# Start of a hybrid encoder trunk on one core: the first weights move to ScalarE's DMA queue, small loads to POOL's, and TensorE's first instructions are put in a written order

## The chip, the cores and the metric

The kernel runs on one core of a Trainium2 chip. The metric is the time of one execution on the device in microseconds (us); where several runs are given, the median counts. A profile of one execution stands beside the times.

## What is computed

Two post-norm layers of an encoder over 512 positions of width 1024. Each layer adds a token mixer and then a squared-ReLU MLP, both with a LayerNorm of `alpha * x + sublayer(x)`. The mixer of the first layer is a bidirectional gated DeltaNet, that of the second a bidirectional GLA.

```python
def reference(x, ...):
    for i in range(DEPTH):                      # DEPTH = 2
        if i % 2 == 0: m = _mixer_gdn(x, a_w_in, a_conv, a_alog, a_dt_bias, a_norm_g, a_w_out)
        else:          m = _mixer_gla(x, b_w_in, ...)
        x = _layernorm(DEEPNORM_ALPHA * x + m, ln1_g[i], ln1_b[i])
        x = _layernorm(DEEPNORM_ALPHA * x + _sq_relu_mlp(x, mlp_w1[i], mlp_w2[i]), ln2_g[i], ln2_b[i])
    return x
```

Only the start of the first mixer matters here. It projects x with `a_w_in` (1024 x 4128): 8 heads with q, k, v and z of 128 columns each, and 32 last columns that give the gates. From these columns come `beta` (a sigmoid) and the decay `g = -exp(a_log) * softplus(. + dt_bias)`; q, k and v go through a short convolution with `a_conv`, and a gated delta rule runs over them in both directions.

## The kernel before, in words

All products of the projections are made in three matmuls of the type fp32r: each operand is split into a high part and the rest (`split`, L85: ScalarE casts `wh`, VectorE subtracts to get `wl`), and `mm3` (L111) adds high x high, high x low and low x high into one bank. x is wanted with its width on the partitions, so its four tiles of 128 positions (`xt`, 512 KB each, rows of 4 KB) are transposed on TensorE (`xpose`, L144 to L156): per tile two banks of four 128 x 128 transposes, then ScalarE's copy to `xth` and VectorE's subtraction to `xtl`. The banks come in turn from the PSUM pools `ac` (2 banks), `ch` (2) and `tp` (1).

`gdn` (L965) first calls `load_x` (L453), which issues the four loads of x on SP and traces the transposes of all four tiles. Then `GdnConst` (L803) is built: triangular masks `cum` on POOL, zeroed tiles `pz` on VectorE, then `gates` (L893). `gates` loads two small broadcasts on ScalarE's queue (`bia` and `coef`, 64 bytes to each partition), the 32 gate columns `bst` (128 KB) and the first head's k columns (512 KB, here called `k0`) on SP's; the splits of both stand behind the last copy of x on their engines (`issue_after`). `proj_halves` (L123) then projects positions 0 to 255 with both sets of weights and afterwards positions 256 to 511: 24 matmuls of 256 columns into the bank `bap` (gates) and 24 into `pjk` (k), per half. Four transposes (`gtp`, L917) and some twenty small operations of VectorE and ScalarE make the gate rows from `bap`. Behind `gates` come the convolution weights `cw` (60 KB, one transpose, L826) and `norm_g` on ScalarE's queue, and masks on POOL that the heads' solves read.

Then the heads are run in a software pipeline: while head i is projected, head i-1 is solved and head i-2 recurs. Head 0's k is already in `pjk`, so the next product is its q (`pjq`), whose weights are the third to be loaded.

What sets the order: a scheduler of the framework places the instructions of each engine at build time, by priority in the order of the program and by what it thinks is ready; each engine then runs its list strictly in order. `in_order` (L58) fixes the order of one engine's instructions within a block to that of the program. Loads of weights go through the pool `wst`, which has three buffers: `bst`, `k0` and the weights of `pjq` fill it, the fourth load waits until `bst` has been split. `c.dma` (L47) always issues on SP.

Of the kernel before, what the change touches and what calls it, by code (L numbers as in the profile page):

```python
# [8 lines left out]
F32 = mybir.dt.float32  # L9
# [3 lines left out]
AF = mybir.ActivationFunctionType  # L13
# [4 lines left out]
P = 128  # L18
S = 512
D = 1024  # L20
KT = D // P
NT = S // P
# [6 lines left out]
class Ctx:  # L29


    def __init__(self, tc, nc, pools):
        self.tc, self.nc = tc, nc
        self.const, self.big, self.wst, self.whl, self.small = pools
        nc_ = nc
        self.ident = self.const.tile([P, P], F32, name="ident")
        make_identity(nc_, self.ident[:, :])

        self.bias = {}
        for i, v in enumerate((LN_EPS, RMS_EPS, -0.5 * math.log(P))):  # L40
            self.bias[v] = self.const.tile([P, 1], F32, name=f"bias{i}")
            nc.vector.memset(self.bias[v], v)
        self.xth = self.xtl = self.xt = None
        self.dma_i = 0
        nc.scalar.preload_act_table_set("natural_log_exp_and_others")
# [78 lines left out]
                     k == 0, k == KT - 1)  # L124
        return ps

    def proj_halves(self, specs):

        out = [self.bank([P, S], F32, name=name, tag=tag) for _, name, tag in specs]
        for hf in range(2):  # L130
            sl = slice(hf * 256, hf * 256 + 256)
            for ps, ((wh, wl), _, _) in zip(out, specs):
                n = wh.shape[-1]
                for k in range(KT):
                    self.mm3(ps[:n, sl], wh[:, k, :], wl[:, k, :], self.xth[:, k, sl], self.xtl[:, k, sl],
                             k == 0, k == KT - 1)
        return out
# [120 lines left out]
def mlp(c, w1, w2, g, b, out=None, extra=None):  # L258
# [12 lines left out]
    with c.banks(pj=2, X=2, Y=2, Z=2), tc.tile_pool(name="mlp", bufs=2) as pool:  # L271
# [176 lines left out]
            second(gi, h, a, nxt)  # L448
            h, a = nh, nxt.a if more else None
        last(G - 1, h)  # L450


def load_x(c, x, tags):  # L453
    c.new_xt()
    c.new_x()
    for t in range(NT):
        c.dma(c.xt[t], x[t * P:(t + 1) * P, :])
    for t in range(NT):
        last = c.xpose(t, c.xt[t], tags)
    return last  # L460


def sel_masks(c, pool, tmp):
# [335 lines left out]
A_H = 8  # L799
# [3 lines left out]
class GdnConst:  # L803


    def __init__(self, c, pool, w_in, a_log, dt_bias, conv_w, norm_g, behind):
        self.c, self.pool = c, pool
        nc = c.nc
        G, V = nc.gpsimd, nc.vector

        self.cum = [pool.tile([P, P], F32, name=f"cum{d}", tag="vn", bufs=9) for d in range(2)]
        for d in range(2):
            self.tri(self.cum[d], d, False, 1.0, 0.0)
        self.ones = pool.tile([P, P], F32, name="ones", tag="vn", bufs=9)
        V.memset(self.ones, 1.0)

        self.pz = {}
        for s in (4, 8, 16, 32, 64):
            self.pz[s] = pool.tile([P, 2 * NT, P], F16, name=f"pz{s}", bufs=1)
            V.memset(self.pz[s], 0.0)  # L820
        self.gates(w_in, a_log, dt_bias, behind)

        cw = pool.tile([120, P], F32, name="cw0", tag="cf", bufs=2)
        nc.scalar.dma_start(cw, conv_w.rearrange("k (t p) -> (k t) p", p=P))
        ps = c.bank([P, P], F32, name="cwp", tag="ch")
        nc.tensor.transpose(ps[:, :120], cw, c.ident[:120, :120])  # L826
        self.cw = pool.tile([P, 5, 24], F32, name="cw", bufs=1)
        V.tensor_copy(self.cw, ps[:, :120].rearrange("p (k t) -> p k t", k=5))
        self.ng = pool.tile([P, 1], F32, name="ng", bufs=1)
        nc.scalar.dma_start(self.ng, norm_g.unsqueeze(1), allow_slow_non_contiguous=True)  # L830
        self.masks()

    def tri(self, t, d, strict, keep, drop):
# [56 lines left out]
        self.ic = pool.tile([P, 4], F16, name="icc", bufs=1)  # L890
        G.tensor_copy(self.ic, ic[:, 0, :])

    def gates(self, w_in, a_log, dt_bias, behind):  # L893

        c, pool = self.c, self.pool
        nc = c.nc
        G, V = nc.gpsimd, nc.vector
        M = 4 * A_H
        H2 = 2 * A_H
        bia = pool.tile([P, H2], F32, name="bia", bufs=1)  # L900
        coef = pool.tile([P, M], F32, name="coef", bufs=1)
        nc.scalar.dma_start(bia, dt_bias.rearrange("d h -> (d h)").partition_broadcast(P))
        nc.scalar.dma_start(coef[:, H2:], a_log.rearrange("d h -> (d h)").partition_broadcast(P))
        st = c.wst.tile([P, KT, M], F32, name="bst", tag="wst")
        b0 = 4 * A_H * P
        c.dma(st, w_in[:, b0:b0 + M].rearrange("(k p) n -> p k n", p=P))
        with c.tc.issue_after(behind.ins):
            wh, wl = c.split(st, [P, KT, M])
            k0 = c.wcols(w_in, A_H * P)
            nc.scalar.activation(coef[:, H2:], coef[:, H2:], AF.Exp)  # L910
        V.memset(coef[:, :H2], 1.0)
        ps, self.k0 = c.proj_halves([((wh, wl), "bap", "ch"), (k0, "pjk", "ac")])
        yr = pool.tile([M, S], F32, name="yr", tag="E", bufs=2)
        nc.scalar.copy(yr, ps[:M, :])
        tps = c.bank([P, NT, P], F32, name="gtp", tag="tp")
        for n in range(NT):
            nc.tensor.transpose(tps[:, n, :M], yr[:, n * P:(n + 1) * P], c.ident[:M, :M])  # L917

        def row(name, tag=None, bufs=1):
            return pool.tile([P, NT, M], F32, name=name, tag=tag or name, bufs=bufs)  # L920

        def bc(t, n):
            return t.unsqueeze(1).to_broadcast([P, NT, n])

        y = row("gy")
        V.tensor_scalar(y[:, :, 0:H2], tps[:, :, 0:H2], -1.0, None, ALU.mult)
        V.tensor_tensor(y[:, :, H2:M], tps[:, :, H2:M], bc(bia, H2), ALU.add)

        e = row("ge", "on", 2)
        nc.scalar.activation(e, y, AF.Abs)  # L930
        nc.scalar.activation(e, e, AF.Exp, scale=-1.0)
        dn = row("gd", "on", 2)
        V.tensor_scalar(dn, e, 2.0, None, ALU.add)
        V.reciprocal(dn, dn)
        V.tensor_tensor(e, e, dn, ALU.mult)
        V.tensor_tensor(dn, e, e, ALU.mult)
        pl = row("gl", "E", 2)
        V.tensor_scalar(pl, dn, -2.0 / 17, None, ALU.mult)
        for n in (15, 13, 11, 9, 7, 5, 3):
            V.scalar_tensor_tensor(pl, pl, -2.0 / n, dn, ALU.add, ALU.mult)  # L940
        V.scalar_tensor_tensor(pl, pl, -2.0, e, ALU.add, ALU.mult)
        V.tensor_scalar(y, y, 0.0, -1.0, ALU.max, ALU.mult)
        V.tensor_tensor(y, y, pl, ALU.add)
        self.last = V.tensor_tensor(y, y, bc(coef, M), ALU.mult)
        self.lnb = y[:, :, 0:H2].rearrange("p n (d h) -> p n d h", d=2)
        gps = c.bank([P, 4, NT, 8], F32, name="gcp", tag="ac")
        for d in range(2):
            src = y[:, :, 16 + 8 * d:24 + 8 * d]
            nc.tensor.matmul(gps[:, d, :, :], self.cum[d], src, start=True, stop=True)
            nc.tensor.matmul(gps[:, 2 + d, :, :], self.ones, src, start=True, stop=True)  # L950
        self.gc = pool.tile([P, NT, 2, 8], F32, name="gc", bufs=1)
        self.tot = pool.tile([P, NT, 2, 8], F32, name="tot", bufs=1)
        for d in range(2):
            V.tensor_copy(self.gc[:, :, d, :], gps[:, d, :, :])
            V.tensor_copy(self.tot[:, :, d, :], gps[:, 2 + d, :, :])

        self.lg = pool.tile([P, NT, 2, 8], F32, name="lg", bufs=1)
        self.tg = pool.tile([P, NT, 2, 8], F32, name="tg", bufs=1)
        V.tensor_tensor(self.lg, self.lnb, self.gc, ALU.subtract)
        V.tensor_tensor(self.tg, self.lg, self.tot, ALU.add)  # L960
        self.egl = pool.tile([P, NT, 2, 8], F32, name="egl", bufs=1)
        nc.scalar.activation(self.egl, self.tot, AF.Exp)


def gdn(c, w_in, conv_w, a_log, dt_bias, norm_g, w_out, ln_g, ln_b, x):  # L965
    tc, nc = c.tc, c.nc
    with c.banks(ch=2, pj=3, tp=1, ac=2), tc.tile_pool(name="gdn", bufs=1) as pool:
        last = load_x(c, x, ("ac", "ch", "tp"))
        g = GdnConst(c, pool, w_in, a_log, dt_bias, conv_w, norm_g, last)
        hi = [c.big.tile([P, 2, S], F32R, name=f"oh{t}", tag=f"xt{t}") for t in range(NT)]  # L970
        lo = [pool.tile([P, S], F32R, name="ol", tag="ol", bufs=A_H) for h in range(A_H)]
        heads = [GdnHead(c, pool, g, h, w_in, hi[h // 2][:, h % 2, :], lo[h]) for h in range(A_H)]
# [437 lines left out]
```

## Time and profile before

| | us |
|---|---|
| median of 3 runs | 1397.46 |
| lowest, highest | 1397.01, 1398.65 |
| the profiled execution | 1397.35 |
| span of its instructions | 1395.6 |
| TensorE busy | 1362.9 |
| VectorE busy | 970.8 |
| ScalarE busy | 701.8 |
| POOL busy | 81.1 |

The span runs from the first to the last instruction of the program; the profiled execution took 1.75 us more than that. All times in views of the trace count from the start of the span. PE is TensorE, ACT ScalarE, DVE VectorE, POOL GpSimd, SP the engine that issues most DMAs; a q behind an engine's name is its queue. "x4" in a row counts instructions merged into it. In the timeline a row begins with start and duration, and the bracket at its end tells how long the engine stood idle and what ended that. The DMA queues are numbered: q1 is SP's, q10 ScalarE's, q0 POOL's.

### The profile page before, as it was taken

Reading aid. Unit: us, or ns where it says so; the run is one execution under the profiler, and the core shown is the slowest. Engines: PE = TensorE matmul, PEld = TensorE weight load, DVE = VectorE, ACT = ScalarE, POOL = GpSimd, SP = SyncE. Lnnn points to the kernel's source line nnn. Section 1 sums busy time; section 2 is a strip of 40 time slices with the busy share of each in tenths; the row PEclk is TensorE's granted clock in tenths of the full one; section 3 lists DMA queues with packets and bytes.
Section 4 is the critical chain, followed back from the end, with each engine's and each line's share of the span. In section 5 each row is a group of like instructions: output and inputs, shape, how many; then the busy total and the mean of one; then the engine's idle time right before and its main releaser. Section 6 shows DMA issues by size and latency. Waiting matters only on the chain.

```text
span 1395.6 us, 20104 instructions
## 1 busy us (share of the span) xinstructions
PE 1362.9 (98%) x7933; PEld 1117.6 (80%) x7933; DVE 970.8 (70%) x1510; ACT 701.8 (50%) x1351; POOL 81.1 (6%) x120
## 2 busy tenths in 40 slices
PE   7999999999999999999999999999999999999997
PEld 6777787777777888888887888888878888888886
DVE  5786787778667677758556587866766657777554
ACT  3776658766743544444542354654434544445430
POOL 5000000000003200000000100000001000000000
PEclk9999999999999999999999999999999999999999
DMA  6321112211232643341131332221216342422121
GB/s 172 76 62 47 46 31 62 61 32 51 72 115 88 207 129 98 92 135 46 48 104 34 93 91 61 61 61 61 92 46 212 110 147 61 136 76 61 46 85 51
DMA packets 146117, 117.05 MB, mean 84 GB/s; under 512 B 7631, under 2 KB 122439, under 8 KB 146023
## 3 DMA queue, kind: packets, MB, share of 16 engines
q1 hardware_dynamic: 144112, 111.49, 26.8%
q0 software_dynamic: 1344, 4.20, 1.0%
q8 instruction: 62, 1.02, 0.3%
q14 instruction: 32, 0.26, 0.1%
q10 hardware_dynamic: 567, 0.08, 0.0%
HBM read 113.66 MB, written 2.10 MB: 83 GB/s over the span
## 4 chain that ended last, share of the span: by engine, by line
PE 63%; issue 25%; ACT 6%; DVE 3%; POOL 2%; DMA 0%; DVEq 0%; POOLq 0%; ACTq 0%
PE pj L115 4%; PE pj L116 4%; PE pj L114 4%; PE pjv L114 3%; PE pjv L115 3%; PE pjv L116 3%; PE scp L685 2%; PE op L1342 2%; PE lv L1216 1%; PE pjq L116 1%; PE pjq L115 1%; PE pjq L114 1%; PE op L773 1%; PE pX L115 1%; PE pX L114 1%
## 5 line engine op out<-in xcount | busy, mean ns | idle before, releaser
L95 ACT CAST wh<-wst 128x1024 fp32r<-128x1024 f32 x137 | 144.0, 1051 | 280.5 <-PE pj L115 164.2
L96 DVE TENSOR_TENSOR wl<-wst,wh 128x1024 fp32r<-128x1024 f32 x137 | 168.4, 1231 | 162.6 <-ACT wh L95 162.0
L116 PE MATMUL pj<-xth,wl 128*128 128x512 f32 (+1 forms) x544 | 201.7, 371 | 0.7 <-DVE wl L96 0.7
L115 PE MATMUL pj<-xtl,wh 128*128 128x512 f32 (+1 forms) x544 | 201.5, 371 | 1.0 <-DVE xtl L155 0.8
L114 PE MATMUL pj<-xth,wh 128*128 128x512 f32 (+1 forms) x544 | 201.3, 371 | 0.0
L96 DVE TENSOR_TENSOR w2l<-w2r,w2h 128x1024 fp32r<-128x1024 f32 x84 | 102.5, 1221 | 49.6 <-ACT w2h L95 49.1
L115 PEld LDWEIGHTS pj<-xtl,wh 128*128 128x128 f32 x544 | 102.4, 188 | 19.2 <-DVE xtl L155 1.4
L116 PEld LDWEIGHTS pj<-xth,wl 128*128 128x128 f32 x544 | 102.3, 188 | 18.7 <-DVE wl L96 0.9
L114 PEld LDWEIGHTS pj<-xth,wh 128*128 128x128 f32 x544 | 102.1, 188 | 18.0 <-ACT xth L154 0.2
L95 ACT CAST w2h<-w2r 128x1024 fp32r<-128x1024 f32 x84 | 88.3, 1051 | 53.3 <-PE pX L116 16.2
L95 ACT CAST ah<-h 128x1024 fp32r<-128x1024 f32 x40 | 42.2, 1054 | 56.2 <-DVE h L357 21.8
L115 PE MATMUL pX<-w2l,ah 128*128 128x512 f32 x144 | 56.1, 390 | 0.0
L114 PE MATMUL pX<-w2h,ah 128*128 128x512 f32 x144 | 56.1, 390 | 0.0
L116 PE MATMUL pX<-w2h,al 128*128 128x512 f32 x144 | 56.1, 390 | 0.0
L114 PE MATMUL pjv<-wh,xth 128*128 128x512 f32 x128 | 54.8, 428 | 0.0
L96 DVE TENSOR_TENSOR al<-h,ah 128x1024 fp32r<-128x1024 f32 x40 | 48.8, 1221 | 2.8 <-ACT ah L95 1.5
L116 PE MATMUL pjv<-wh,xtl 128*128 128x512 f32 x128 | 50.2, 392 | 0.0
L115 PE MATMUL pjv<-wl,xth 128*128 128x512 f32 x128 | 49.9, 390 | 0.0
L163 ACT ACTIVATE rsy<-bmv,bias 128x1 f32<-128x1 f32 x16 | 4.7, 294 | 82.4 <-DVE bmv L192 82.4
L114 PE MATMUL pjk<-xth,wh 128*128 128x512 f32 (+1 forms) x112 | 41.6, 372 | 0.6 <-ACT wh L95 0.6
L116 PE MATMUL pjk<-xth,wl 128*128 128x512 f32 (+1 forms) x112 | 41.5, 370 | 0.0
L114 PE MATMUL pjq<-xth,wh 128*128 128x512 f32 (+1 forms) x104 | 40.6, 391 | 0.9 <-DVE xt L322 0.9
(439 smaller groups left out, 3448.4 us busy)
## 6 DMA issues: line engine op xcount, KB each, us to landing
wst<-in_mlp_w SPq DMA_DIRECT2D x80, 512.0 KB, 4.0
w2r<-in_mlp_w SPq DMA_DIRECT2D x48, 512.0 KB, 3.7
wst<-in_a_w_in SPq DMA_DIRECT2D x32, 512.0 KB, 4.1
wst<-in_b_w_in SPq DMA_DIRECT2D x32, 256.0 KB, 3.0
wst<-in_a_w_out SPq DMA_DIRECT2D x8, 512.0 KB, 3.9
wst<-in_b_w_in SPq DMA_DIRECT2D x8, 512.0 KB, 3.8
wst<-in_b_w_out SPq DMA_DIRECT2D x8, 512.0 KB, 3.6
xt<-in_x SPq DMA_DIRECT2D x4, 512.0 KB, 7.3
```

Of the source, the lines that this page charges most:

```text
L95: nc.scalar.copy(hi, src)
L96: nc.vector.tensor_tensor(lo, src, hi.bitcast(F32), ALU.subtract)
L114: mm(ps, ah, bh, start=start, stop=False, **kw)
L115: mm(ps, ah, bl, start=False, stop=False, **kw)
L116: mm(ps, al, bh, start=False, stop=stop, **kw)
L163: nc.scalar.activation(y, x, AF.Ln, bias=self.bias[eps])
L685: T.matmul(ps[:, n, :], kh[:, sl], qh[:, sl], start=True, stop=True)
L773: T.matmul(ops, l, r, start=i == 0, stop=i == len(mm) - 1)
L1216: T.matmul(ps[:, u, :, :], lhs[:, u, :], cols(rhs, u, s, i), start=True, stop=True)
L1342: T.matmul(op[:, n, :], l, r, start=i == 0, stop=i == len(mm) - 1)
```

## The change

- The loads of `bst` and `k0` are issued first of all, on ScalarE's queue; the four loads of x stay on SP's. `load_x` goes away.
- The four small loads (`bia`, `coef`, `cw`, `norm_g`) move from ScalarE's queue to POOL's.
- Within `in_order` for TensorE stand now: 14 transposes of the identity into a bank that nobody reads (`idle`, in the pool `pj`), the 8 transposes of the first tile of x, 4 idle ones, the 8 of the second tile, 6 idle ones, the first half of the projection (all of `bap`, then all of `pjk`), the 16 transposes of the third and fourth tile, the second half.
- The splits of `bst` and `k0` stand behind the copies of the second tile of x, no longer behind those of the fourth.

```diff
-    def proj_halves(self, specs):
+    def proj_halves(self, specs, between=None):
...
         for hf in range(2):
+            if hf and between:
+                between()
...
-def load_x(c, x, tags):
-    c.new_xt()
-    c.new_x()
-    for t in range(NT):
-        c.dma(c.xt[t], x[t * P:(t + 1) * P, :])
-    for t in range(NT):
-        last = c.xpose(t, c.xt[t], tags)
-    return last
...
     def __init__(self, c, pool, w_in, a_log, dt_bias, conv_w, norm_g, x):
...
+        st = c.wst.tile([P, KT, 4 * A_H], F32, name="bst", tag="wst")
+        k0 = c.wst.tile([P, KT, P], F32, name="wst", tag="wst")
+        c.new_xt()
+        c.new_x()
+
+        def tiles(ts):
+            for t in ts:
+                c.dma(c.xt[t], x[t * P:(t + 1) * P, :])
+
+        b0 = 4 * A_H * P
+        nc.scalar.dma_start(st, w_in[:, b0:b0 + 4 * A_H].rearrange("(k p) n -> p k n", p=P))
+        nc.scalar.dma_start(k0, w_in[:, A_H * P:A_H * P + P].rearrange("(k p) n -> p k n", p=P))
+        tiles(range(NT))
...
-        nc.scalar.dma_start(cw, conv_w.rearrange("k (t p) -> (k t) p", p=P))
+        nc.gpsimd.dma_start(cw, conv_w.rearrange("k (t p) -> (k t) p", p=P))
...
-        nc.scalar.dma_start(self.ng, norm_g.unsqueeze(1), allow_slow_non_contiguous=True)
+        nc.gpsimd.dma_start(self.ng, norm_g.unsqueeze(1), allow_slow_non_contiguous=True)
...
-        nc.scalar.dma_start(bia, dt_bias.rearrange("d h -> (d h)").partition_broadcast(P))
-        nc.scalar.dma_start(coef[:, H2:], a_log.rearrange("d h -> (d h)").partition_broadcast(P))
-        st = c.wst.tile([P, KT, M], F32, name="bst", tag="wst")
-        b0 = 4 * A_H * P
-        c.dma(st, w_in[:, b0:b0 + M].rearrange("(k p) n -> p k n", p=P))
-        with c.tc.issue_after(behind.ins):
-            wh, wl = c.split(st, [P, KT, M])
-            k0 = c.wcols(w_in, A_H * P)
-            nc.scalar.activation(coef[:, H2:], coef[:, H2:], AF.Exp)
+        nc.gpsimd.dma_start(bia, dt_bias.rearrange("d h -> (d h)").partition_broadcast(P))
+        nc.gpsimd.dma_start(coef[:, H2:], a_log.rearrange("d h -> (d h)").partition_broadcast(P))
+        def xposes(ts):
+            for t in ts:
+                last = c.xpose(t, c.xt[t], ("ac", "ch", "tp"))
+            return last
+
+        with c.in_order(mybir.EngineType.PE):
+            idle = c.bank([P, NT, P], F32, name="idle", tag="pj")
+
+            def turn(n):
+
+                for i in range(n):
+                    nc.tensor.transpose(idle[:, i % NT, :], c.ident, c.ident)
+
+            turn(14)
+            xposes((0,))
+            turn(4)
+            behind = xposes((1,))
+            turn(6)
+            with c.tc.issue_after(behind.ins):
+                st = c.split(st, [P, KT, M])
+                k0 = c.split(k0, [P, KT, P])
+                nc.scalar.activation(coef[:, H2:], coef[:, H2:], AF.Exp)
+            ps, self.k0 = c.proj_halves([(st, "bap", "ch"), (k0, "pjk", "ac")], lambda: xposes((2, 3)))
         V.memset(coef[:, :H2], 1.0)
-        ps, self.k0 = c.proj_halves([((wh, wl), "bap", "ch"), (k0, "pjk", "ac")])
```

More of the change, by code (lines that the diff above doesn't have):

```diff
@@ L803, with __init__ @@
 class GdnConst:
-    def __init__(self, c, pool, w_in, a_log, dt_bias, conv_w, norm_g, behind):
+    def __init__(self, c, pool, w_in, a_log, dt_bias, conv_w, norm_g, x):
         self.c, self.pool = c, pool
@@ L820, in __init__ @@
             V.memset(self.pz[s], 0.0)
-        self.gates(w_in, a_log, dt_bias, behind)
+        self.gates(st, k0, a_log, dt_bias)
         cw = pool.tile([120, P], F32, name="cw0", tag="cf", bufs=2)
-        nc.scalar.dma_start(cw, conv_w.rearrange("k (t p) -> (k t) p", p=P))
+        nc.gpsimd.dma_start(cw, conv_w.rearrange("k (t p) -> (k t) p", p=P))
         ps = c.bank([P, P], F32, name="cwp", tag="ch")
@@ L891, in masks, with gates @@
         G.tensor_copy(self.ic, ic[:, 0, :])
-    def gates(self, w_in, a_log, dt_bias, behind):
+    def gates(self, st, k0, a_log, dt_bias):
         c, pool = self.c, self.pool
@@ L967, in gdn @@
     with c.banks(ch=2, pj=3, tp=1, ac=2), tc.tile_pool(name="gdn", bufs=1) as pool:
-        last = load_x(c, x, ("ac", "ch", "tp"))
-        g = GdnConst(c, pool, w_in, a_log, dt_bias, conv_w, norm_g, last)
+        g = GdnConst(c, pool, w_in, a_log, dt_bias, conv_w, norm_g, x)
         hi = [c.big.tile([P, 2, S], F32R, name=f"oh{t}", tag=f"xt{t}") for t in range(NT)]
```

## The prediction

> **What bounds the kernel now.** I read the page first, then the chain of work that ended last, then the timeline of the first 30 us, then the DMA view of that stretch.
>
> ```profile
> span 1395.6 us, 20104 instructions
> ...
> PE 1362.9 (98%) x7933; PEld 1117.6 (80%) x7933; DVE 970.8 (70%) x1510; ACT 701.8 (50%) x1351; POOL 81.1 (6%) x120
> ...
> PE 63%; issue 25%; ACT 6%; DVE 3%; POOL 2%; DMA 0%; DVEq 0%; POOLq 0%; ACTq 0%
> ```
>
> TensorE is busy 98% of the span: only 1395.6 - 1362.9 = 32.7 us without it. The change touches the start, and there the chain reads:
>
> ```profile
> 11.93 1.56 ACT xth L154 x3
> 13.49 1.33 ACT wh L95 x2
> 14.86 0.39 PE pjk L114
> ...
> 26.25 0.36 PE gtp L917 x4
> ```
>
> Copies of x, the two weight splits, then matmuls of `pjk` and `bap` without a break up to the `gtp` transposes. From there TensorE stays full (the chain goes on with `pjq`), so what moves the end of this first projection moves the end of the kernel by as much. The quantity to forecast is when `gtp` starts: 26.18 now. Its parts, from the timeline:
>
> ```profile
> 6.10 4.04 PE L151 MATMUL tp<-ident,xt 128*128 128x128 f32 x18 [6.10 <-POOL blk L873]
> ...
> 11.26 1.50 PE L151 MATMUL tp<-ident,xt 128*128 128x128 f32 x12 [0.91 <-DVE xtl L155]
> ...
> 12.55 1.89 DVE L155 TENSOR_TENSOR xtl<-tp,xth 128x512 fp32r<-128x512 f32 x3 [0.68 <-ACT xth L154]
> ...
> 13.37 0.43 ACT L95 CAST wh<-bst 128x256 fp32r<-128x256 f32 x1
> ...
> 13.76 1.05 ACT L95 CAST wh<-wst 128x1024 fp32r<-128x1024 f32 x1
> ...
> 14.84 1.23 DVE L96 TENSOR_TENSOR wl<-wst,wh 128x1024 fp32r<-128x1024 f32 x1
> ...
> 20.48 0.28 PE L114 MATMUL bap<-xth,wh 128*32 128x256 f32 x1
> ...
> 23.21 0.28 PE L114 MATMUL pjk<-xth,wh 128*128 128x256 f32 x1
> ...
> 25.97 0.28 PE L116 MATMUL pjk<-xth,wl 128*128 128x256 f32 x1
> 26.18 0.43 PE L917 MATMUL gtp<-ident,yr 32*128 32x32 f32 x4
> ```
>
> Second half of the projection: 20.48 to 26.18 = 5.70 us, of it 24 `bap` matmuls 2.73 (0.114 each) and 24 `pjk`, 23 steps in 2.76 (0.12 each). From the start of the cast of the `k0` weights to both their parts being there: 13.76 to 14.84 + 1.23 = 2.31 us. From a first transpose to the end of the third `xtl`: 11.26 to 12.55 + 1.89 = 3.18 us.
>
> Now the transfers:
>
> ```profile
> 0.81 1.81 SPq L50 DMA_DIRECT2D xt<-in_x  x4
> ...
> 5.98 0.38 SPq L50 DMA_DIRECT2D bst<-in_a_w_in  x1
> ...
> 6.40 0.79 SPq L50 DMA_DIRECT2D wst<-in_a_w_in  x1
> ...
> 7.93 2.84 SPq L50 DMA_DIRECT2D wst<-in_a_w_in  x1
> ```
>
> Their times from issue to landing, first and last tile of x, then the two `wst`:
>
> ```profile
> xt<-in_x SPq DMA_DIRECT2D x1, 512.0 KB, 5.2
> ...
> xt<-in_x SPq DMA_DIRECT2D x1, 512.0 KB, 8.9
> ...
> wst<-in_a_w_in SPq DMA_DIRECT2D x1, 512.0 KB, 7.3
> ...
> wst<-in_a_w_in SPq DMA_DIRECT2D x1, 512.0 KB, 7.5
> ```
>
> x lands from 0.81 + 5.2 = 6.0 to 2.2 + 8.9 = 11.1, `k0` at 6.40 + 7.3 = 13.7 (its cast starts at 13.76), the next weights, `pjq`'s (call them q), at 7.93 + 7.5 = 15.4. SP issued `bst` as the ninth hardware DMA (four of x, four small ones on ScalarE's queue), and not before the first tile of x had landed: eight are let out, the ninth waits.
>
> ```profile
> 2.00:4.00 2.00, 0.00 (x0) 0.00 (x0) 1.72 (x6) 0.09 (x1) 1.81 (x9) 1.00 0.44 155
> 4.00:6.00 2.00, 0.00 (x0) 0.00 (x0) 0.00 (x0) 0.00 (x0) 1.74 (x5) 1.00 0.71 206
> 6.00:8.00 2.00, 1.90 (x9) 1.61 (x9) 0.16 (x1) 0.59 (x1) 0.35 (x2) 1.00 0.86 311
> 8.00:10.00 2.00, 2.00 (x12) 1.88 (x12) 1.50 (x3) 1.22 (x3) 0.00 (x0) 1.00 1.05 384
> 10.00:12.00 2.00, 1.09 (x11) 0.88 (x10) 1.71 (x3) 1.10 (x3) 0.00 (x0) 1.00 1.22 252
> 12.00:14.00 2.00, 0.92 (x9) 0.66 (x7) 1.45 (x3) 2.00 (x5) 0.00 (x0) 1.00 1.21 289
> ```
>
> In this table of stretches the column before the last is the DMA engines' busy share: full from 8 us on, 0.44, 0.71 and 0.86 before. Unused are 2 x (0.56 + 0.29 + 0.14) = 1.98 us. So earlier issues can win at most about 2 us for the whole set of transfers.
>
> **The change part by part.** *The two rings.* How the queues share the 16 engines decides what comes first. Packets of SP's ring (q1) and ScalarE's (q10), from 2.8 to 7 us and from 7.5 to 9.5:
>
> ```profile
> q1 hardware_dynamic: 247, 0.91, 64.9%
> q10 hardware_dynamic: 233, 0.01, 3.1%
> ...
> q1 hardware_dynamic: 200, 0.75, 91.8%
> q10 hardware_dynamic: 194, 0.06, 11.5%
> ```
>
> One for one, though x's packets are 4 KB rows and the others 4 to 512 bytes. In the changed kernel ScalarE's ring holds `bst` (128 KB in 128-byte rows, 1024 packets, 64 per engine) and behind it `k0` (512 KB in 512-byte rows, again 64). x has 512 rows, 32 per engine. When x is done, half of `bst` is. And q: `wst` has three buffers and only six hardware DMAs are out before it, so q is issued on SP right behind x, at about 2.6 instead of 7.93. Its 64 packets per engine then pair with the rest of `bst` and with the first half of `k0`. The last to land is `k0`, where it was q. The bytes are the same, so `k0` lands between 15.4 - 2.0 = 13.4 and 15.4; it landed at 13.7. Cross-check, 11 to 13 us, 512-byte rows alone:
>
> ```profile
> q1 hardware_dynamic: 1123, 0.56, 121.0%
> ```
>
> 16 engines x 2 us / 1123 = 0.0285 us a packet; after x come 64 of q and 64 of `k0`, 3.65 us, and 32 small ones of `bst`, at most 0.9.
>
> *The four small loads go to POOL's queue.* Broadcasts hold up a ring beside them. The weights' ring alone (447.5 to 449 us), then with POOL's ring (q0) beside it (449.5 to 451):
>
> ```profile
> q1 hardware_dynamic: 196, 0.40, 79.5%
> ...
> q0 software_dynamic: 44, 0.18, 68.9%
> q1 hardware_dynamic: 28, 0.05, 9.2%
> ```
>
> 196 packets fall to 28 in the same 1.5 us. The slow first 7 us are, I think, the `bia` and `coef` broadcasts at work on x. On POOL they start later, behind the `cum` masks:
>
> ```profile
> 2.08 0.29 POOL L837 TENSOR_SCALAR_AFFINE_SELECT cum<-cum 128x128 f32<-128x128 f32 x1
> ```
>
> so x runs undisturbed for a while after 2.4 us, and is then held as before. Of the 1.98 us I take 1.3 as won: `k0` lands at 14.1. The extra issues on POOL delay its masks, which nobody reads before the first solve, a whole head's projection later; if that cover failed, the solve would wait for POOL, which is busy 81 us in all. `cw` and `bia` are first read behind the projection.
>
> *TensorE's order written down.* Before, `bap` and `pjk` of the first half filled each other's waits. Now it is: transposes of x0 and x1, first half of `bap`, of `pjk`, transposes of x2 and x3, second half. Behind `pjk`'s wait for `k0` stand x2 and x3, which have landed by then, and all that follows. `bap` needs `bst`: at latest 1.8 us after x (32 + 32 packets), some 11.8, plus 0.43 and 0.41 for its split, so it ends by 12.7 + 2.73 = 15.4, while `k0` is split at 14.1 + 2.3 = 16.4: hidden, with 1 us to spare. Then 22 `pjk` matmuls that need the low part, 22 x 0.12 = 2.64. Then 16 transposes; the second half reads what the third `xtl` of them gives, 3.18 us, in which TensorE mostly stands: a stall that the old order did not have. Then 5.70.
>
> *Idle transposes.* 14 + 4 + 6, each 0.21 us cold or 0.11 warm (4.04 us for 18, 1.50 for 12). They lie in TensorE's wait for x and the weights: nothing. The spacing halves after a stretch that held transposes alone, while the granted-clock column (1.00 in every stretch above) does not show it. The page TensorE: Matmul & The Clock Gate of the Trainium skill (Part 4: PE-mode transpose) says that transposes do not count as activity that opens the clock; this trace contradicts it, so the idle ones can do their work. By the page the first `bap` matmuls would run cold and the time be that of the third rival below, 1400.5; by the trace it is the sum.
>
> **Sum.** `gtp` starts at 14.1 + 2.31 + 2.64 + 3.18 + 5.70 = 27.9, against 26.18: +1.8 us. The profiled execution took 1397.35 us, so 1399.1; the median of the runs shown, 1397.46, is 0.1 above it, less than any step here is sure to. With `k0` at 13.4 or 15.4 the sum gives +1.1 or +3.1.
>
> **Rivals.** *Weights arrive with x1* (several small rows are served for each row of x). For: in the counts above each partition had one row of a transfer; `bst` and `k0` have eight, and how eight are served beside x the trace does not show. Against: the counts themselves. Then x1 sets the start. By even steps between 6.0 and 11.1 it lands at 7.7, and at 5.7 with all the slack won. Its two copies are through 3.18 - 0.6 (one step of 1.89 / 3) later, at 10.3, and with the split of `bst` (0.41) `bap` runs from 10.7; 10.7 + 2.73 + 2.88 + 3.18 + 5.70 = 25.2, -1.0 us; from 5.7, -3.0. Time 1394.4 to 1396.4.
>
> *Slower: POOL's broadcasts hold all three rings to the end of x*, and nothing of the slack is won. Place: the rings until x lands; price: `k0` at 15.4 and +3.1 us, 1400.4. It decides for slower once `k0` lands after 15.1.
>
> *The clock closes again*: x1 at 7.7, its 8 transposes and 6 idle ones at 0.11 end at 9.2; `bap` starts at 12.2: TensorE stands for 3 us. Before, it stood 0.91 us (the bracket at 11.26) and came back warm; a wait of 3 us is not among the rows here. At half speed `bap` takes 5.5 us instead of 2.73 and ends at 17.8 instead of being hidden behind 16.4: 1.4 us more, 1400.5. The same page (Part 1: The HAM clock gate) has an idle window of about 3.4 us close the gate, just above these 3; no run here shows it.
>
> *Nothing moves* because the gate arithmetic behind `gtp`, not TensorE, paces what follows: 1397.4. Against it: `pjq` fills TensorE right behind `gtp`.
>
> **How the numbers follow.** 0.2% of this kernel, 2.8 us, is about what a measurement tells from no change. Forecast 0.50; weights with x1 0.20, half of it past the bound; held rings 0.17; cold clock 0.08; nothing moves 0.05. Faster 0.10, slower 0.17 + 0.08 = 0.25, the same 0.65. The range takes in the early-weights rival up to 1394.8 and the slow ones with a further 1.3 us of re-ordering behind the start, 1401.8. The forecast's own range is 1398.4 to 1400.4.
>
> **What would show it.** `k0` lands after x's last tile, near 14; q's issue at 2.6; counts of both rings equal until x is done; a TensorE gap ahead of `pjk`'s first low-part matmul and another of 1 to 2 us behind the x2 and x3 transposes; `gtp` near 28. `k0` landed by 10 would break the forecast at its root; a `gtp` near 28 with an unchanged end would break the step that carries the start to the end.

## The result, and the profile after

The changed kernel takes 1402.63 us (median of 6 runs, 1401.81 to 1403.5), the kernel before beside it 1397.34 (6 runs): a ratio of 1.0034, 95% interval 1.0024 to 1.0045. Measured again beside the experiments it was 1402.06 against 1397.17, 1.0032 (1.0019 to 1.0044). The forecast was 1399.1 and its range ended at 1401.8. The profiled execution took 1401.92, 4.57 us more than the profiled one of before. Two executions of the kernel before, at 2250 and 3422 us in the last round of experiments, are left out of the ratios. The page of the profile:

```profile
span 1400.2 us, 20163 instructions
...
PE 1368.4 (98%) x7957; PEld 1122.4 (80%) x7957; DVE 973.1 (69%) x1510; ACT 701.9 (50%) x1351; POOL 83.4 (6%) x124
```

TensorE is not idle longer than before (1400.2 - 1368.4 = 31.8 us against 32.7): the idle transposes count as busy, and so do matmuls at half clock. The page can't show the loss; the timeline of TensorE over the first 31 us does:

```profile
1.53 3.25 PE L922 MATMUL idle<-ident 128*128 128x128 f32 x14 [1.53 <-POOL ident masks.py:199]
4.92 1.97 PE L154 MATMUL tp<-ident,xt 128*128 128x128 f32 x8
...
8.47 0.82 PE L922 MATMUL idle<-ident 128*128 128x128 f32 x6
9.66 0.30 PE L114 MATMUL bap<-xth,wh 128*32 128x256 f32 x1 [0.37 <-ACT wh L95]
...
15.95 0.38 PE L114 MATMUL pjk<-xth,wh 128*128 128x256 f32 x1 [2.69 <-ACT wh L95]
17.21 0.38 PE L116 MATMUL pjk<-xth,wl 128*128 128x256 f32 x1 [0.76 <-DVE wl L96]
21.45 1.47 PE L154 MATMUL tp<-ident,xt 128*128 128x128 f32 x12
23.45 0.66 PE L154 MATMUL tp<-ident,xt 128*128 128x128 f32 x4 [0.53 <-DVE xtl L158]
24.64 0.31 PE L115 MATMUL bap<-xtl,wh 128*32 128x256 f32 x1 [0.19 <-DVE xtl L158]
30.25 0.43 PE L939 MATMUL gtp<-ident,yr 32*128 32x32 f32 x4
```

`gtp` starts at 30.25 instead of 26.18. `bap` starts at 9.66 (13.85 before), and this wins nothing: `pjk` waits for `k0`, whose cast ScalarE starts after 5.25 us of waiting for the transfer:

```profile
9.19 0.42 ACT L95 CAST wh<-bst 128x256 fp32r<-128x256 f32 x1
14.86 1.04 ACT L95 CAST wh<-wst 128x1024 fp32r<-128x1024 f32 x1 [5.25 <-DMA wst<-in_a_w_in]
```

From 17.21 to 21.45 the first half of `pjk` takes 4.24 us where 2.64 were forecast. The table of stretches says why (the first number behind a stretch's length is the busy time of TensorE; the last three are the granted clock, the DMA engines' share and GB/s):

```profile
6.00:9.00 3.00, 3.00 (x22) 2.83 (x21) 1.53 (x3) 1.94 (x4) 2.32 (x7) 1.00 1.06 152
...
14.00:18.00 4.00, 1.29 (x8) 1.09 (x9) 2.07 (x2) 2.10 (x3) 0.00 (x0) 0.98 0.53 129
18.00:21.00 3.00, 3.00 (x16) 3.00 (x16) 0.29 (x1) 0.00 (x0) 0.00 (x0) 0.50 0.92 230
```

The clock is at 0.50 in the whole stretch from 18 to 21, after one in which TensorE worked 1.29 of 4 us. And from 6 to 9 us the DMA engines are counted as busy throughout, yet move only 152 GB/s. Packets by queue, from 3.5 to 4.5, from 6 to 9 and from 9 to 12 us:

```profile
q10 hardware_dynamic: 956, 0.12, 77.3%
q1 hardware_dynamic: 49, 0.15, 39.2%
...
q0 software_dynamic: 54, 0.02, 59.1%
q1 hardware_dynamic: 91, 0.35, 36.5%
q10 hardware_dynamic: 156, 0.08, 10.8%
...
q1 hardware_dynamic: 411, 0.74, 69.1%
q10 hardware_dynamic: 410, 0.21, 24.9%
```

First `bst` runs ahead of x, 956 packets to 49; then 54 packets of POOL's ring (q0, the small loads, the `bia` and `coef` broadcasts among them) are counted with 59% of 16 engines for 3 us, while the two other rings move little; then, with `k0`'s 512-byte rows beside the last rows of x and the first of q, the rings go one for one.

The end of the kernel moves by 4.57 us, `gtp` by 4.07. Behind `gtp` TensorE now waits where it did not wait before, for VectorE's gate arithmetic. The row of `gcp` (the gates' running sums), before and without a bracket, then the timeline of TensorE after:

```profile
41.19 0.38 PE L949 MATMUL gcp<-gy,cum 128*128 128x32 f32 x2
```

```profile
30.61 0.32 PE L833 MATMUL cwp<-ident,cw 120*128 120x120 f32 x1
...
47.97 0.38 PE L971 MATMUL gcp<-gy,cum 128*128 128x32 f32 x2 [1.13 <-DVE gy L966]
```

### The profile page after: what moved, and what is told of

It reads as the page before. It is cut to its first block, busy times and chain, and to the rows that moved or that the text cites. A ratio compares the mean times of both kernels' runs of the same rounds, so it can differ in the third digit from the quotient of the medians.

```text
span 1400.2 us, 20163 instructions
## 1 busy us (share of the span) xinstructions
PE 1368.4 (98%) x7957; PEld 1122.4 (80%) x7957; DVE 973.1 (69%) x1510; ACT 701.9 (50%) x1351; POOL 83.4 (6%) x124
## 4 chain that ended last, share of the span: by engine, by line
PE 61%; issue 25%; ACT 6%; DVE 5%; POOL 2%; DMA 1%; DVEq 0%; POOLq 0%; ACTq 0%
PE pj L116 4%; PE pj L115 4%; PE pj L114 4%; PE pjv L114 3%; PE pjv L116 3%; PE pjv L115 3%; PE scp L678 2%; PE op L1363 2%; PE lv L1237 1%; PE op L766 1%; PE pX L116 1%; PE pjq L114 1%; PE pX L115 1%; PE pX L114 1%; PE pjq L115 1%
## 5 line engine op out<-in xcount | busy, mean ns | idle before, releaser
L115 PE MATMUL pjk<-xtl,wh 128*128 128x512 f32 (+1 forms) x112 | 42.1, 376 | 0.0
```

Of the source, the lines that this page charges most:

```text
L115: mm(ps, ah, bl, start=False, stop=False, **kw)
```

## The experiments

Each time stands beside runs of the kernel before on the same chip, whose medians were 1397.17 to 1397.50. Diffs are against the changed kernel unless another is named. The expectations name the theories by letters. A: POOL's broadcasts hold the rings (in *queues_only*: the new queues make `k0` and x late). B: the third weights (q) halve the rate of `k0`. C is the clock in *warm*, and from *gates_first* on the stall that the written order has behind x2 and x3; that stall is called D in *order_only*. From *own_buf* on, D is that POOL's masks disturb VectorE, and E that VectorE's list alone makes the wait.

| kernel | what is different | median us | ratio to before (95%) |
|---|---|---|---|
| late_small | small loads held until x3 has landed | 1398.98 | 1.0014 (1.0005, 1.0023) |
| late_q | q's load held until `k0`'s cast | 1400.99 | 1.0027 (1.0017, 1.0036) |
| warm | 24 idle transposes ahead of `pjk` | 1400.48 | 1.0023 (1.0013, 1.0032) |
| warm_more | 36 of them | 1400.37 | 1.0017 (1.0008, 1.0025) |
| order_only | loads of before, order of after | 1400.03 | 1.0019 (1.001, 1.0028) |
| queues_only | loads of after, order of before | 1401.0 | 1.0024 (1.0015, 1.0034) |
| gates_first | all of `bap` ahead of `pjk` | 1402.5 | 1.0033 (1.002, 1.0045) |
| gates_first_late | and small loads late | 1401.84 | 1.003 (1.0018, 1.0042) |
| acts | gates_first, casts behind the copies of x | 1398.02 | 1.0 (0.9991, 1.0008) |
| acts_late | and small loads late | 1398.02 | 1.0 (0.9991, 1.0009) |
| acts_all | and third and fourth weights late | 1399.74 | 1.0011 (1.0002, 1.002) |
| own_buf | another buffer for `cw` | 1401.29 | 1.0028 (1.0017, 1.004) |
| own_warm | warm_more, another buffer | 1399.06 | 1.001 (1.0001, 1.0019) |
| own_best | acts_late, another buffer | 1395.37 | 0.9982 (0.9973, 0.9991) |
| cw_late | before, `cw`'s transpose late | 1398.86 | 1.0013 (1.0004, 1.0022) |

**What holds `k0` back.** *late_small* makes POOL copy one element per partition of x's last tile ahead of the four small loads:

```diff
+        hold = pool.tile([P, 1], F32, name="hold", bufs=1)
+        self.hold = G.tensor_copy(hold, c.xt[3][:, 0:1])
...
+        with c.tc.issue_after(self.hold.ins):
+            nc.gpsimd.dma_start(bia, dt_bias.rearrange("d h -> (d h)").partition_broadcast(P))
```

> The changed kernel, with the four small loads held on POOL until the last tile of x has landed. Theory A (the two broadcasts on POOL's queue hold the other rings and make k0 late): k0 lands near 11 instead of 14.8, TensorE waits for it less than 1.5 us and stays warm, gtp starts near 25 instead of 30.25, and the time is about 5 us below the changed kernel, some 1396.5 to 1397.5. Theory B (the third weights' load q, issued early on SP, takes k0's turns): k0 still lands after 13, gtp starts after 28, and the time is above 1400.

Its table of stretches from 6 to 9 us, and its timeline of TensorE:

```profile
6.00:9.00 3.00, 3.00 (x22) 2.90 (x20) 1.68 (x3) 2.09 (x4) 0.00 (x0) 1.00 1.05 380
```

```profile
13.59 0.39 PE L114 MATMUL pjk<-xth,wh 128*128 128x256 f32 x1 [0.47 <-ACT wh L95]
14.84 0.39 PE L116 MATMUL pjk<-xth,wl 128*128 128x256 f32 x1 [0.76 <-DVE wl L96]
17.59 1.47 PE L154 MATMUL tp<-ident,xt 128*128 128x128 f32 x12
```

Same busy share, 380 GB/s instead of 152. `k0`'s cast starts at 12.49 instead of 14.86, TensorE waits only 0.47 + 0.76 us, the clock stays open in this execution (five of the eleven took 1399.7 or more, with a lower mean clock), and the first half of `pjk` takes 17.59 - 14.84 = 2.75. `gtp` starts at 26.43, 0.25 later than before, yet the end is later by 1.2 (1398.58 against 1397.35 in the profiled executions): something behind `gtp` costs as well. So `k0` came 1.5 us later and the time 1.5 us higher than theory A had them. That POOL's small loads hold the rings is shown; which of the four does it is not, since they were held together.

*late_q* lets ScalarE write one element per partition of q's tile after `k0`'s cast, so that SP's load waits for it:

```diff
-    def wcols(self, w, c0, n=P, pool=None):
+    def wcols(self, w, c0, n=P, pool=None, after=None):
...
+        if after is not None:
+            self.nc.scalar.copy(st[:, 0, 0:1], after[:, 0, 0:1].bitcast(F32))
```

> The changed kernel, but the third weights (q) are issued on SP only once the cast of k0 has begun to release them (ScalarE writes one element of q's tile first); the four small loads stay early on POOL. Theory A (POOL's broadcasts hold the rings): from 6 to 9 us the rings still move about 150 GB/s, and k0 lands at 13.5 or later, since 1.3 us at most of q's bytes stood in its way. Theory B (q's 512 KB pair with k0 packet by packet): k0 lands at 12.5 or earlier, as soon as x and bst are through plus half a transfer, the clock stays open through pjk, and gtp starts at 27 or earlier against 30.25. In either case q lands near 18, which pjq does not feel before gtp.

`k0`'s cast starts at 13.72, against 14.86 and 15.15 in the two profiles of the changed kernel: 1.1 to 1.4 us, as theory A had it. But SP issued the fourth weights at 10.33 in q's place, as soon as `bst` was split, and they paired with `k0` in its stead. *acts_all*, below, holds both.

**The changed kernel again.**

> The changed kernel once more beside these three on the same chip: 1402.6 within 0.8, gtp at 30.2, the granted clock at 0.50 for one stretch of 3.4 us while the first half of pjk runs.

1402.06, `gtp` at 30.57, and the clock at 0.50 from 18 to 21: as expected.

**The clock.** *warm* and *warm_more* put idle transposes between the first halves of `bap` and `pjk`, 24 and 36 (shown with 36):

```diff
-            for ps, ((wh, wl), _, _) in zip(out, specs):
+            for j, (ps, ((wh, wl), _, _)) in enumerate(zip(out, specs)):
...
+                if fill and hf == 0 and j == 1:
+                    fill()
...
-            ps, self.k0 = c.proj_halves([(st, "bap", "ch"), (k0, "pjk", "ac")], lambda: xposes((2, 3)))
+            ps, self.k0 = c.proj_halves([(st, "bap", "ch"), (k0, "pjk", "ac")], lambda: xposes((2, 3)), lambda: turn(36))
```

> The changed kernel, with 24 more idle transposes between the first halves of bap and pjk, where TensorE stood 2.7 us. Theory C (the wait for k0 let the clock fall to half, and 16 matmuls of pjk ran at 0.213 us instead of 0.12): the slow stretch goes, gtp starts 1.5 us earlier, near 28.7, and the time is 1.5 us below the changed kernel, about 1401. Rival: transposes do not keep the clock up, or the clock fell for another reason; then the slow stretch stays and the time is that of the changed kernel, 1402.6, or a little above it.

> The changed kernel with 36 idle transposes between the first halves of bap and pjk, 36 x 0.107 = 3.9 us, where 24 left TensorE idle from 12.2 to 15.0 in the profiled execution. Theory (the halved clock is what a stretch with too few matmuls leaves behind): no stretch with doubled steps in pjk, gtp near 30.25 - 1.6 = 28.6, the time about 2 us under the changed kernel, 1400.0 to 1400.6, and this in all executions, not in 8 of 10. Rival (the clock falls for another reason, the load of the engines with transfers say): steps of 0.21 us in pjk again, and 1401.8 to 1402.6.

With 24, eight of ten executions had a mean clock of 0.998 or more and took 1400.0 to 1400.7; in the other two, of which the profiled one is one, the clock fell as without them. With 36 none of the eleven has a mean clock under 0.998: all took between 1400.08 and 1400.81. TensorE and stretches of *warm_more*:

```profile
12.56 4.09 PE L924 MATMUL idle<-ident 128*128 128x128 f32 x36
...
19.79 1.47 PE L156 MATMUL tp<-ident,xt 128*128 128x128 f32 x12
...
28.59 0.43 PE L941 MATMUL gtp<-ident,yr 32*128 32x32 f32 x4
```

```profile
15.00:18.00 3.00, 2.83 (x26) 2.62 (x23) 2.21 (x2) 1.81 (x3) 0.00 (x0) 1.00 0.28 66
18.00:21.00 3.00, 3.00 (x29) 3.00 (x27) 0.15 (x1) 0.57 (x2) 0.00 (x0) 1.00 0.95 244
```

`gtp` moves from 30.25 to 28.59, 1.66 us. `k0` is almost as late as in the changed kernel (cast at 14.71 instead of 14.86); the 22 matmuls take 19.79 - 17.07 = 2.72 instead of 4.24. That the idle stretch ahead of `pjk` closes the clock, and that this costs 1.5 us, is shown.

**The two halves of the change.** *order_only* issues `bst` and `k0` on SP behind x and the small loads on ScalarE's queue, as before, and keeps the new order; *queues_only* keeps the new queues, without `in_order` and idle transposes, x transposed ahead of the projection.

> TensorE's written order and the idle transposes of the changed kernel, but all loads as in the kernel before: x, bst and k0 on SP, the four small ones on ScalarE's queue. k0 should land at 13.7 as before. Theory D (the written order itself costs the 3.2 us stall behind the late transposes of x): with a warm clock gtp starts at 13.76 + 2.35 + 2.64 + 3.19 + 5.61 = 27.5, 1.3 us later than before, time 1398.7; if the clock falls during the wait for bst (from about 9.5 to 12.4), up to 1.5 us more, 1400.2. Rival (the queues are the whole cost, the order none): time as before, 1397.3.

> The loads on the queues of the changed kernel, but TensorE's order left to the scheduler, all transposes of x ahead of the projection, no idle transposes. Theory A (queues make k0 late, 14.8 instead of 13.7, and x late, 12.6 instead of 11.1): gtp starts 1.1 to 1.5 us later than before, near 27.5, time about 1398.6. If the order were the whole cost: as before, 1397.3, or faster. If the queues were the whole cost: near the changed kernel, 1402.

Each alone costs 2.8 to 3.8 us; together 5. *queues_only* took 2.4 us more than expected. In its profile TensorE is at half speed until 20.2: the last 12 transposes take 2.80 us where the changed kernel's take 1.47, and `bap` goes in steps of 0.21, though the granted-clock column reads 1.00. Why it speeds up so late is not shown. TensorE of *order_only*:

```profile
12.36 0.42 PE L114 MATMUL bap<-xth,wh 128*32 128x256 f32 x1 [2.64 <-ACT wh L95]
...
28.14 0.43 PE L939 MATMUL gtp<-ident,yr 32*128 32x32 f32 x4
```

Here `bst` lands only behind x, the 2.64 us of waiting close the clock (0.50 from 12 to 15), and `bap` runs at half speed: the third rival to the letter, though only where the queues are not changed. In *queues_only* `gtp` starts at 30.18, 4.0 us later than before, and the span is 1399.3, 3.7 us longer: nothing is lost behind `gtp` there. In *order_only* `gtp` is 2.0 us later and the span 3.3 longer. So the loss behind `gtp` comes with the written order.

**Filling the wait with the gates.** *gates_first* runs all of `bap`, with the transposes of x2 and x3 inside it, ahead of `pjk`; *gates_first_late* holds the small loads too (`part` is the loop of `proj_halves` for one set of weights and one half).

```diff
-            ps, self.k0 = c.proj_halves([(st, "bap", "ch"), (k0, "pjk", "ac")], lambda: xposes((2, 3)))
...
+            part(ps, st, 0, range(4))
+            xposes((2,))
+            part(ps, st, 0, range(4, KT))
+            xposes((3,))
+            part(ps, st, 1, range(KT))
+            part(self.k0, k0, 0, range(KT))
+            part(self.k0, k0, 1, range(KT))
```

> The changed kernel with its queues, but TensorE's written order is: first half of bap up to chunk 3, transposes of x2, rest of the first half of bap, transposes of x3, second half of bap, then both halves of pjk. Theory C (after the landing of k0 the written order costs the 3.2 us stall behind x2 and x3, because pjk stands ahead of them): k0 lands near 14.8 as before, the stall is gone, pjk ends 2.31 + 48 x 0.12 = 8.1 us after k0's landing, at 23 to 24, and gtp, which waits for bap alone, starts far before that; the end comes 5 or 6 us earlier than in the changed kernel, near 1396. Rival: ScalarE's list places the casts of k0 and q and the exp ahead of the copies of x2 and x3, so the second half of bap waits for k0 all the same, and the gain is under 2 us.

> The order of gates_first with the four small loads held back on POOL until x3 has landed. k0 lands near 12.5 as it did with the small loads held alone; pjk's two halves end at 12.5 + 2.3 + 5.8 = 20.6, 5.5 us ahead of the kernel before. Theory C: the end comes 3 to 5 us ahead of before, 1392 to 1394.5, less some 1 us of re-ordering. Rival (ScalarE's list makes the copies of x2 and x3 wait for k0): no faster than 1397.

The rival won in both. ScalarE of *gates_first* has the copies of x2 and x3 behind the casts of `k0` and q:

```profile
15.31 1.04 ACT L95 CAST wh<-wst 128x1024 fp32r<-128x1024 f32 x1 [4.70 <-DMA wst<-in_a_w_in]
...
16.38 1.03 ACT L95 CAST wh<-wst 128x1024 fp32r<-128x1024 f32 x1
17.32 1.55 ACT L157 CAST xth<-tp 128x512 fp32r<-128x512 f32 x3
```

The changed kernel has the same list; an order written for TensorE alone leaves ScalarE's in the scheduler's hands. *acts* moves the split of `k0` and the exp behind the last copy, *acts_late* holds the small loads too, *acts_all* also the third and fourth weights (diff against *gates_first*):

```diff
-            xposes((3,))
+            last = xposes((3,))
             part(ps, st, 1, range(KT))
+            with c.tc.issue_after(last.ins):
+                k0 = c.split(k0, [P, KT, P])
...
+                nc.scalar.activation(coef[:, H2:], coef[:, H2:], AF.Exp)
```

> Queues of the changed kernel; TensorE's order bap, x2, bap, x3, second half of bap, then pjk; and on ScalarE the casts of k0 and q and the exp behind the copies of x2 and x3. Theory C (the stall behind x2 and x3 is the price of the written order): with x3 landed at 12.6, the second half of bap runs from about 15.2 to 17.9, k0 landed at 15 is split by 17.4, pjk ends at 17.9 + 5.8 = 23.7, 2.5 us ahead of before; time 1395 plus some 1 us of re-ordering, 1395 to 1396.5. Rival (something else paces the start, or the re-ordering behind it takes the gain back): 1397.5 or more.

> acts with the four small loads held back on POOL until x3 has landed. x3 at 10.2, k0 at 12.5, second half of bap from about 13 to 15.7, pjk to 21.6, 4.5 us ahead of before. Theory C: 1393 plus 1 us of re-ordering, 1393 to 1394.5. Rival (the re-ordering behind it takes it back): 1397 or more.

> acts_late, and the loads of the third and fourth weights (q and v) are held on SP until k0's cast, so that nothing stands beside k0 once x is through. Theory B (k0 is halved by the weights of SP's ring): k0 lands at 11 to 11.5, a microsecond and more ahead of 12.5. Since bap's second half ends at 15.7 whatever k0 does, the time is that of acts_late within 0.5. Theory that the fourth load stands in for q where q alone is held: q's load alone won 1.4 us of 15.1, both together win more. Rival: k0 still at 12.5, the engines are then at their limit with x alone.

`gtp` starts at 24.29, 23.84 and 24.11, some 2 us ahead of before, and yet no time is below before: *acts* and *acts_late* can't be told from it, *acts_all* is 2.2 us above. The start is won and given back behind it, as the rivals of *acts* and *acts_late* had it. In *acts_all* `k0` lands at 11.3 (issued at 1.32) against 12.4 in *acts_late*, so q and the fourth weights did cost it 1.1 us; its packets from 9 to 12 us show the ring with little beside it:

```profile
q10 hardware_dynamic: 525, 0.26, 32.2%
q1 hardware_dynamic: 23, 0.06, 5.1%
```

Its time missed the expectation by 1.7. TensorE waits 2.99 us ahead of `gcp` instead of 1.49: ScalarE casts the weights held back at 21.42 and 23.23 instead of 15.99 and 18.08, VectorE subtracts for them up to 25.5, and the gate arithmetic starts at 25.45 instead of 24.31. This execution took 1398.04, 1.4 us more than the profiled one of *acts_late*; seven others took 1399.5 to 1401.3 with a mean clock of 0.997 or less, so the clock fell in them as well.

**What takes it back.** TensorE's wait ahead of `gcp` shows it in all of these (1.13 us in the changed kernel, 1.48 in *acts*). Before, POOL waited for the transpose of `cw`, because `cw`'s buffer is one of two that its masks use; the scheduler had slipped that transpose between the first `pjk` matmuls. POOL of before, then TensorE of before:

```profile
15.54 0.21 POOL L869 MEMSET blk<- 128x128 f32 x1 [9.12 <-PE cwp L826]
```

```profile
15.21 0.27 PE L826 MATMUL cwp<-ident,cw 120*128 120x120 f32 x1
```

In the changed kernel it was not slipped in: `cwp` comes at 30.61, behind `gtp`, and POOL waits 22.23 us. The written order does not forbid it (a `pjq` matmul stands inside it, at 24.06); why the scheduler left `cwp` so late is not shown. One candidate is its bank: of the two of pool `ch`, `bap` holds one and the transposes of x2 and x3 use the other. POOL's masks then run beside the gate arithmetic. POOL after, and VectorE after at the same time:

```profile
31.00 0.20 POOL L876 MEMSET blk<- 128x128 f32 x1 [22.23 <-PE cwp L833]
...
37.98 2.13 POOL L886 TENSOR_TENSOR off<-blk 128x512 f16<-128x512 f32 x1
```

```profile
38.88 1.37 DVE L962 SCALAR_TENSOR_TENSOR gl<-gl,gd 128x128 f32<-128x128 f32 x1
```

An operation of 0.28 us ends 0.14 after POOL's. The group of this line on VectorE (count, busy us, mean ns), before, after and in *own_buf*:

```profile
L940 DVE SCALAR_TENSOR_TENSOR gl<-gl,gd 128x128 f32<-128x128 f32 x7 | 1.9, 278 | 0.0
```

```profile
L962 DVE SCALAR_TENSOR_TENSOR gl<-gl,gd 128x128 f32<-128x128 f32 x7 | 3.3, 465 | 0.0
```

```profile
L962 DVE SCALAR_TENSOR_TENSOR gl<-gl,gd 128x128 f32<-128x128 f32 x7 | 1.9, 278 | 0.0
```

The page SBUF — State Buffer of the Trainium skill (SBUF: two separate sides) says that VectorE and GpSimd share one pair of ports as an exclusive lock, that a VectorE operation with two inputs in SBUF needs it against a GpSimd operation that reads SBUF, and that the one that starts later blocks; these rows agree. *own_buf* takes the wait away with a buffer of another tag; the lists of TensorE and VectorE stay the same. *own_warm* and *own_best* do it in *warm_more* and *acts_late*. *cw_late* puts the wait into the kernel before (the edit of *own_buf*, then that of *cw_late*):

```diff
-        cw = pool.tile([120, P], F32, name="cw0", tag="cf", bufs=2)
+        cw = pool.tile([120, P], F32, name="cw0", tag="vn", bufs=9)
```

```diff
+        with c.tc.issue_after(self.gtp.ins):              # cw_late, on the kernel before
+            nc.tensor.transpose(ps[:, :120], cw, c.ident[:120, :120])
```

> The changed kernel, with the convolution weights in another pool's buffer, so that POOL's masks no longer wait for their transpose; the lists of TensorE and VectorE stay as they are. Theory D (masks beside the gate arithmetic stretch it): POOL's masks run from 9 to 23 us, the gate operations of VectorE take 5.6 us instead of 7.3 and 15.4 from first to last instead of 17.1, the wait of 1.13 us ahead of gcp is gone, and the time is 0.6 to 1.1 us under the changed kernel, 1401.5 to 1402. Rival E (VectorE's list alone): gate operations still 17 us from first to last, the wait stays, 1402.6.

> warm_more (36 idle transposes, the clock stays open) and the other buffer for the convolution weights. Theory D: gtp near 28.6 as in warm_more, no wait ahead of gcp, so the end is late by what gtp is late, 2.4 us: 1397.4 + 2.4 = 1399.8 or a little less, against 1400.4. Rival E: 1400.4.

> acts_late (small loads late, all of bap ahead of pjk, copies of x ahead of k0's cast) and the other buffer for the convolution weights. Theory D: gtp near 23.8, the gate arithmetic from 24.3 to 39, TensorE's wait ahead of gcp under 0.8 us and no halved clock behind it, so that 1.5 to 2.3 of the 2.3 us are kept: 1395 to 1396. Rival E: the wait of 1.5 us stays, 1397 to 1398.

> The kernel before with one edit: the transpose of the convolution weights is issued behind the gtp transposes. Theory D: POOL's masks wait until 26.9 and run to 41, the gate operations of VectorE are stretched from 5.6 to over 7 us, TensorE waits 1 us or more ahead of gcp where it did not wait at all, and the time rises by 1 to 1.5 us, or by 2.5 to 3 where the clock falls behind the wait: 1398.4 to 1400.4. Rival E: no change beyond 0.3 us, 1397.4.

All four went as theory D had them, *own_buf* and *own_warm* a little better than expected (1401.29, 1399.06), *own_best* and *cw_late* within their ranges (1395.37, 1398.86). TensorE of *own_buf*, with no bracket left, then of *own_best*, then of *cw_late*:

```profile
46.69 0.38 PE L971 MATMUL gcp<-gy,cum 128*128 128x32 f32 x2
```

```profile
23.85 0.43 PE L961 MATMUL gtp<-ident,yr 32*128 32x32 f32 x4
...
38.59 0.38 PE L993 MATMUL gcp<-gy,cum 128*128 128x32 f32 x2
```

```profile
43.85 0.38 PE L950 MATMUL gcp<-gy,cum 128*128 128x32 f32 x2 [1.48 <-DVE gy L945]
```

The profiled execution of *cw_late* (1400.17) has a second loss: the clock falls ahead of `gtp`, which starts at 27.59. Stretches of *cw_late*, then of before:

```profile
12.00:16.00 4.00, 2.36 (x19) 1.77 (x18) 3.43 (x5) 3.47 (x7) 0.00 (x0) 1.00 0.74 178
16.00:20.00 4.00, 4.00 (x24) 3.38 (x22) 1.24 (x2) 0.46 (x1) 0.00 (x0) 0.58 1.06 268
```

```profile
12.00:16.00 4.00, 2.33 (x18) 1.75 (x17) 3.38 (x6) 3.48 (x7) 0.40 (x2) 1.00 0.74 179
16.00:20.00 4.00, 4.00 (x37) 3.90 (x35) 1.53 (x3) 0.50 (x1) 3.65 (x6) 1.00 1.07 265
```

Up to 16 us the two are almost the same, so this loss comes and goes with the execution. The times show it in both kernels: *cw_late* has six executions at 1398.7 to 1398.9 and five at 1400.1 to 1400.4, before has 20 at 1397.0 to 1397.8 and seven at 1398.5 to 1399.3 beside them. Both groups moved by 1.3 to 1.4.

So one late transpose is worth 1.3 to 1.4 us with everything else held (1400.37 to 1399.06; 1397.48 to 1398.86), and 2.65 in *acts_late* (1398.02 to 1395.37). There the clock also falls in a part of the executions: the five of *acts_late* with a mean clock of 0.998 or more took 1396.7 to 1397.2, 1.6 above *own_best*, the six others 1398.0 to 1399.2. That it falls behind the wait is seen in the profile of *acts* (0.67 in its stretch from 40 to 44). *own_best* beats both kernels: 1395.37 against 1397.48, ratio 0.9982 (0.9973 to 0.9991).

## Why the prediction was wrong

The direction inside its own range was right (+1.8 forecast), the size was not (+5.3). Step by step:

- **`k0` lands at 14.1**: it landed at about 14.85, inside the bounds 13.4 to 15.4 that the step gave. "Of the 1.98 us I take 1.3 as won" failed in size: POOL's small loads hold the rings for 3 us, worth 2.4 us of `k0` (*late_small*); that rival, kept apart at 1400.4, was half of the truth.
- **One for one** failed for `bst`: eight rows per partition of 128 bytes were served some 20 to one row of x (956 to 49). The rival that saw this, weights with x1, was right on `bst` (split from 9.19) and wrong on the result, since `k0` comes last either way. For `k0`'s 512-byte rows the step held (411 to 410).
- **The split, 2.31**: 17.21 - 14.86 = 2.35, right.
- **22 `pjk` matmuls, 2.64**: 4.24. This is the step that failed by most. I asked whether the clock closes while TensorE waits for `bap`, priced it there, and found `bap` hidden; it was hidden, by 3.9 us instead of 1, and that is the point: `bap` was through early, so the wait moved to `pjk`, 2.69 + 0.76 us, in front of the chain. The sum had `pjk` start right behind a wait of its own ("a TensorE gap ahead of `pjk`'s first low-part matmul") and did not ask what that gap does to the clock. Worth 1.5 (*warm_more*).
- **The stall behind x2 and x3, 3.18**: 24.64 - 21.45 = 3.19, right; and so is the **second half, 5.70**: 30.25 - 24.64 = 5.61.
- These make 30.25 of 27.93: 0.76 for `k0`, 1.60 for the 22 matmuls at half clock, -0.04 for the rest.
- **What moves the end of the projection moves the end of the kernel by as much**: by 0.5 us more in the profiled executions. "`cw` and `bia` are first read behind the projection" was false: the row `15.54 ... [9.12 <-PE cwp L826]` was in the trace of before, on an engine that I had put aside as 6% busy. "If that cover failed, the solve would wait for POOL" looked for the price in the wrong place: the masks were not late for their readers, they were in VectorE's way. Worth 1.3 (*own_warm*). Without that wait the end is less late than `gtp`, by 0.5 us in the profiled executions of *own_buf* and 0.7 of *own_warm*; where that comes from stays open.
- **Idle transposes cost nothing**: right. And they do count for the clock: 36 of them kept it at 1.00 (*warm_more*).

The rivals were priced one at a time, each from a sound rest. Two of them, the held rings and the clock, came together, the clock at another place, and a third mechanism with them; the range had room for one and 1.3 us of re-ordering.

## What to carry to other kernels

An order written down for one engine can cost what the scheduler had slipped into its gaps: list those instructions and who waits for each, through shared buffers too, before the order is fixed, and look at what the other engines' lists do with the new order. Where a wait is moved, price the clock at its new place. And where rivals don't exclude one another, the range has to hold their sum.

## What the runs showed of the hardware

- While POOL's queue had its small loads under way (two of the four are broadcasts), its packets were counted with 0.591 x 16 x 3 / 54 = 0.53 us of an engine each, and all rings together moved 152 GB/s instead of 380.
- The clock fell for 3.4 us (in the changed kernel's steps of 0.21 us from 17.9 to 21.3) after stretches in which TensorE was busy for a third to little more than half: in the 3.4 us ahead of the fall 1.19 us in the changed kernel, 1.83 in *warm*, 1.76 in *cw_late*, 1.92 in *acts*. In *warm* no single wait in that stretch was longer than 0.9 us. In *warm_more*, with 3.00 of 3 us from 12 to 15, almost all transposes, and 2.83 of 3 from 15 to 18, it stayed open. Neither the busy share nor the length of a wait decides alone: the kernel before, busy for 1.73 us in the stretch of *cw_late*, kept its clock, and so did *acts_all* over its wait of 2.99 us, each in the profiled execution. What else decides is open. The page TensorE: Matmul & The Clock Gate of the Trainium skill (Part 1: The HAM clock gate) has one idle window of about 3.4 us close it: the length agrees with the stretch at half speed, the condition is stricter than what these runs show.
